# Three edits to a planned kernel: longer planned latencies, mixer loads nine blocks sooner, and a first pair of tiles that runs one tile alone on ten weight slabs

## The chip, the cores and the metric

The kernel runs on all eight cores of one Trainium2 chip. Each core works on one sequence of the batch, and nothing is exchanged between the cores. The metric is the time of one execution on the device, in microseconds (us), of the slowest core.

Executions come in two states. Most are "fast". In some, the cores of one die or of both are granted a lower TensorE clock, and the run is some per cent longer (in the slow run of after one die has 0.960 to 0.965, the other 0.993 to 0.995, and the time is 2481.05 instead of 2411 us; in one run of g2_best_try all eight cores have 0.816 to 0.824, and it takes 2861.9 instead of 2386 us); those are called slow and are left out of every comparison. In some runs that count as fast, two or more cores have a mean granted clock of about 0.98 instead of 0.989 to 0.998, and the run is 10 to 30 us longer. I call those runs "disturbed". I quote the ratio of the fast runs and, beside it, the undisturbed times alone.

## The reference

One layer of a decoder block, for 8 sequences of 4096 positions and width 1024. Every sublayer is modulated by shift, scale and gate rows that come from a conditioning vector `c`.

```python
D_MODEL, BATCH, SEQ, D_FF = 1024, 8, 4096, 2816
def swiglu_ffn(h, w_in, w_out):
    gate, up = jnp.split(h @ w_in, 2, axis=-1)
    return (jax.nn.silu(gate) * up) @ w_out

mod = silu(c) @ w_mod + b_mod                     # 9 rows: sh1, sc1, gt1, sh2, sc2, gt2, sh3, sc3, gt3
h = ada_rmsnorm(x, g_ffn1, sh1, sc1)
x = x + 0.5 * gt1 * swiglu_ffn(h, w_ffn1_in, w_ffn1_out)      # first FFN
h = ada_rmsnorm(x, g_mix, sh2, sc2)               # mixer: conv of width 31 beside a linear recurrence
...                                               # (cut)
x = x + gt2 * (concat(y_conv, y_rnn) @ w_out)
h = ada_rmsnorm(x, g_ffn2, sh3, sc3)
x = x + 0.5 * gt3 * swiglu_ffn(h, w_ffn2_in, w_ffn2_out)      # second FFN
return ada_rmsnorm(x, g_final, f_shift, f_scale)
```

## The kernel before

The sequence is cut into 8 tiles of 512 positions. The first FFN runs on pairs of tiles (pairs 0 to 3), so that each weight slab (128x2048 bf16, 512 KB) serves two tiles. Then each tile runs its mixer and its second FFN.

**A planner of its own.** The kernel lists every operation with a duration and a priority. A list scheduler simulates the engines with these numbers and so fixes, once and for all, the order of instructions on each engine and which buffer each value gets. At run time the engines only follow that order and wait on semaphores. A number such as `DMA_LAT` is thus no delay; it only moves operations in the order. The argument `after` in the listings also acts in the plan alone; `sync` makes an engine wait at run time.

```python
D_CAST, D_SLAB, D_CHUNK, D_PREP = 2.7, 1.65, 0.85, 4.6   # planned us of one DMA channel
DMA_LAT = 2.0
SEM_LAT = 0.08
...
        if op.nbytes:
            ...
                c = max(s + dur, chan[0]) + op.nbytes
                chan[0] = c
                op.end = c + DMA_LAT
        else:
            et[e] = s + sw + dur
            op.end = s + sw + dur + SEM_LAT
...
        for q in op.succ:
            q.ndep -= 1
            q.ready = max(q.ready, op.end if op in q.deps else s)
```

**Weights arrive as fp32.** In pair 0 each slab of `w1i` and `w1o` is loaded by a casting DMA (issued by GpSimd) into one of 10 slab slots, and then written back as bf16 to HBM by a DMA of SyncE; later pairs load the bf16 copy. The weights `w2o` are cast in the same way in the second FFN of tile 0. The others are converted from HBM to HBM during pairs 1 to 3 (the list `prep`).

```python
        def load_slab(nm, r, cast, prio=None, after=(), sync=()):
            b = new(sl, f"{nm}{r}")
            if cast:
                dma("PL", lambda: b.ap, lambda: src, D_CAST, ..., sync=sync)      # cast into the slot
                dma("SP", lambda: d.ap, lambda: b.ap, D_SLAB, ...)                # write back as bf16
            else:
                dma("SP", lambda: b.ap, lambda: d.ap, D_SLAB, ...)
```

**The modulation rows use the same slots.** Eight loads of `wmod` (512 KB each) and eight VectorE operations make one group of eight modulation rows. The groups of sh1 and sc1 come at the start; the VectorE operations of the gate's group (gt1) are planned for after block 8 of pair 0, while its loads are issued as slots come free.

```python
        def mods(m, afters):
            for q in range(8):
                b = new(sl, f"mod{m + q}")
                dma("SP", ..., slab=True, prio=P.prio)                            # wmod row block
                last = A("DVE", 1.3, f, [crow], [b, modr[m]], after=(afters[q],))
...
            for j in range(FC):                                                   # FC = 22 blocks
                slab = load_slab("w1i", j, pi == 0, sync=() if pi else (mod_ops[M_SH1 + 2 * j] if j < 2 else xss[-1][3 if j == 2 else 7].lw,),
                                 after=[xb.lw for xb in xss[-1]] if pi == 0 and j >= 2 else ())
                ops = ffn_in(slab, hbs, hids, j, split=(j == 0))
                anchors.append((pi, ops[-1]))
                if pi == 0 and j == 8:
                    gt_anchor = ops[-1]
...
        def mix_ffn2(t):
            gate_op = (last_in, anchors[-2][1])[t] if t < 2 else ffn_anchor[t - 2]
            xs = load_x(xm_dr, t, after=(gate_op,) * 8)
            ...                                                                   # mixer (cut)
            for j in range(FC):
                slab = load_slab("w2i", j, False)
                ops = ffn_in(slab, [hb2], [hid], j)
            ffn_anchor[t] = ops[-1]
```

`ffn_in` issues, for each tile of the pair, 8 matmuls into a "gate" bank and 8 into an "up" bank of PSUM; ScalarE takes the first bank through SiLU, and a VectorE multiply (`hid`) reads both.

## Time and profile before

| | before |
|---|---|
| time, median of 4 fast runs | 2409.31 us (2407.95 to 2412.9) |
| spans of the eight cores, profiled run | 2386.8 to 2405.7 us |
| TensorE busy, slowest core | 2318.5 us, 96% |

The page of the kernel before begins with the busy time of each engine. Then come 40 equal slices of the span; each digit is the busy share in tenths. "PEclk" is the granted clock.

```profile
span 2405.7 us, 35029 instructions; the slowest of 8 cores (2386.8 to 2405.7 us)
...
PE 2318.5 (96%) x11346; PEld 1110.4 (46%) x11346; DVE 1183.6 (49%) x2019; ACT 931.4 (39%) x1394; POOL 111.2 (5%) x213
...
PE   1999999999999999999899999999999999999997
...
DMA  9999599679867766464976555555555555555455
...
PE 87%; DMA 6%; ACT 3%; DVE 2%; issue 2%; SPq 1%; ACTq 0%; DVEq 0%; POOLq 0%
```

TensorE bounds the kernel: it is busy 96% of the span, and the chain of waits (last line) is 87% matmul. Where the granted clock is 1.00, a 128x512 matmul starts every 0.216 us. What can be won are the few stretches in which TensorE idles or is granted a clock of 0.50 (on core 0, for instance, from 59.5 to 66.2 us, where the matmuls start every 0.427 us), and the chain of the slowest core (core 0) names them. Its columns are start, duration, and what the chain passed through:

```profile
49.84 10.78 DMA sb_slab<-w1i
60.76 115.10 PE ps L443 x520
176.81 39.96 DMA sb_c<-x
...
1182.85 11.17 DMA sb_c<-xmid
```

There are three DMA waits to read here: the third weight slab near 50 us, x of the second pair near 217 us, and x of the third tile's mixer near 1185 us. The waits of TensorE on the same core (total us, times, longest) show the same from TensorE's side; `sb_h` stands for what VectorE makes of the loaded x, and also for the `hid` products:

```profile
PE ps L443 <- DVE sb_h L423: 37.0, 15, 12.4
PE ps L443 <- ACT sb_h L401: 28.9, 2, 28.7
...
PE ps L443 <- DVE sb_c L409: 4.3, 6, 0.8
...
PE ps L443 <- DMA sb_slab<-w1i: 2.9, 1, 2.9
```

For comparing kernels I use one measure that I worked out from the traces, **TensorE's loss** at a time t: the time elapsed minus 0.216 us for each 128x512 matmul and 0.109 us for each 128x256 matmul started so far. It adds up idle time and slow clock and says in which stage they arose. I give its median over those cores of the profiled run whose trace holds all 11346 matmuls and whose clock is at least 0.985. Before, it stands at 55.2 us at 82 us (the start, 45 us, is in it), grows by 5.1 from 82 to 300 us, and by 21.3 from 300 to 2200 us.

### The profile page before, as it was taken

How to read it: one execution, taken by the hardware profiler on the slowest of the kernel's cores; microseconds unless marked ns; L12 is line 12 of the kernel's file. 1: busy time of each engine (PE TensorE's matmuls, PEld its weight loads, DVE VectorE, ACT ScalarE, POOL GpSimd, SP SyncE). 2: the span in 40 equal slices, each digit the busy share in tenths (PEclk: the TensorE clock that was granted, in tenths of full speed). 3: DMA queues.
4: the chain of work that ended last, by engine and by line, in shares of the span. 5: the costliest groups of instructions: out<-in, count | busy, mean ns of one | idle time of the engine just before them, and what ended most of it. 6: DMA issues, size and time to landing. Idle time of an engine off the chain costs nothing.

```text
span 2405.7 us, 35029 instructions; the slowest of 8 cores (2386.8 to 2405.7 us)
## 1 busy us (share of the span) xinstructions
PE 2318.5 (96%) x11346; PEld 1110.4 (46%) x11346; DVE 1183.6 (49%) x2019; ACT 931.4 (39%) x1394; POOL 111.2 (5%) x213
## 2 busy tenths in 40 slices
PE   1999999999999999999899999999999999999997
PEld 0444444444444445454354454454454454454446
DVE  6334133523352337585285385484484584574223
ACT  3214011401131116466265365364364364374222
POOL 0010100010010000000000000000000000000000
PEclk9999999999999999999999999999999999999999
DMA  9999599679867766464976555555555555555455
GB/s 274 226 210 240 176 218 220 166 197 221 218 173 188 187 178 206 153 214 149 225 187 221 189 180 188 187 181 185 191 177 191 186 183 185 186 182 188 162 184 184
DMA packets 135106, 466.64 MB, mean 194 GB/s; under 512 B 16368, under 2 KB 18544, under 8 KB 134256
## 3 DMA queue, kind: packets, MB, share of 16 engines
q1 hardware_dynamic: 117216, 386.54, 49.7%
q0 software_dynamic: 17712, 77.87, 17.3%
q8 instruction: 95, 1.56, 0.3%
q14 instruction: 83, 0.68, 0.1%
HBM read 453.07 MB, written 79.69 MB: 221 GB/s over the span
## 4 chain that ended last, share of the span: by engine, by line
PE 87%; DMA 6%; ACT 3%; DVE 2%; issue 2%; SPq 1%; ACTq 0%; DVEq 0%; POOLq 0%
PE ps L443 87%; DMA sb_c<-x 2%; ACT sb_c L401 2%; DMA sb_c<-xmid 2%; SPq L450 1%; DMA sb_slab<-wmod 1%; DVE sb_c L423 1%; DMA sb_slab<-w1i 0%; DVE sb_c L749 0%; DVE sb_c L409 0%; ACT L401 0%; DVE sb_h L423 0%; DVE sb_c L419 0%; DVE sb_ub L419 0%; DVE sb_c L429 0%
## 5 line engine op out<-in xcount | busy, mean ns | idle before, releaser
L443 PE MATMUL ps<-sb_h,sb_slab 128*128 128x512 bf16 (+1 forms) x10160 | 2178.2, 376 | 31.8 <-ACT sb_h L401 28.9
L443 PEld LDWEIGHTS ps<-sb_h,sb_slab 128*128 128x128 bf16 x10160 | 995.9, 98 | 1195.9 <-issue 44.6
L423 DVE TENSOR_TENSOR sb_h<-ps,sb_c 128x512 bf16<-128x512 f32 x352 | 241.4, 691 | 769.4 <-PE ps L443 708.6
L401 ACT ACTIVATE sb_c<-ps 128x512 f32<-128x512 f32 x400 | 236.5, 596 | 868.0 <-PE ps L443 864.5
L423 DVE TENSOR_TENSOR sb_c<-sb_c 128x512 f32<-128x512 f32 (+1 forms) x492 | 308.8, 672 | 115.6 <-ACT sb_c L401 113.0
L401 ACT ACTIVATE sb_c<-sb_c 128x512 f32<-128x512 f32 (+1 forms) x329 | 198.5, 616 | 263.0 <-DVE sb_c L419 183.3
L401 ACT ACT_TABLE_LOAD x106 | 136.0, 1283 | 224.7 <-PE ps L443 202.4
L419 DVE SCALAR_TENSOR_TENSOR sb_c<-ps,sb_gth,sb_c 128x512 f32<-128x512 f32 (+1 forms) x136 | 96.7, 717 | 212.0 <-PE ps L443 211.6
L401 ACT ACTIVATE sb_h<-sb_c,sb_modv,sb_gs 128x512 bf16<-128x512 f32 x151 | 108.9, 801 | 38.5 <-DVE sb_modv L423 24.9
L443 PE MATMUL ps<-sb_ub,sb_slab 128*128 128x256 bf16 x1024 | 115.0, 273 | 4.9 <-DVE sb_c L409 4.3
L443 PEld LDWEIGHTS ps<-sb_ub,sb_slab 128*128 128x128 bf16 x1024 | 99.5, 98 | 22.1 <-issue 8.7
L500 DVE SCALAR_TENSOR_TENSOR sb_slab<-sb_slab,sb_crow 128x1024 f32<-128x1024 f32 x88 | 107.1, 1217 | 3.4 <-DMA sb_slab<-wmod 2.4
L450 POOL DMA_DIRECT2D y<-sb_c x56 | 30.3, 542 | 1012.9 <-ACT sb_c L401 864.1
L423 DVE TENSOR_TENSOR sb_h<-sb_c 128x512 bf16<-128x512 f32 (+1 forms) x98 | 65.8, 678 | 21.8 <-ACT sb_c L401 19.6
L419 DVE SCALAR_TENSOR_TENSOR sb_c<-sb_ux,sb_vecs,sb_c 128x512 f32<-128x512 f32 x96 | 69.6, 746 | 1.7
L443 PE MATMUL ps<-sb_h,sb_ones 128*128 128x512 bf16 (+1 forms) x98 | 34.4, 382 | 37.3 <-DVE sb_h L423 37.0
L419 DVE SCALAR_TENSOR_TENSOR sb_c<-ps,sb_modv,sb_c 128x512 f32<-128x512 f32 x64 | 47.9, 749 | 31.0 <-PE ps L443 31.0
L419 DVE SCALAR_TENSOR_TENSOR sb_ub<-sb_c,ps 64x256 bf16<-64x256 f32 x128 | 53.8, 420 | 15.1 <-PE ps L443 11.6
L450 POOL DMA_DIRECT2D xmid<-sb_c x64 | 35.0, 547 | 361.6 <-DVE sb_c L419 357.8
L401 ACT ACTIVATE sb_c<-sb_c,sb_lam 128x512 f32<-128x512 f32 x64 | 50.0, 821 | 0.5
L409 DVE TENSOR_SCALAR sb_c<-ps,sb_vecs 64x256 f32<-64x256 f32 x85 | 40.7, 484 | 8.9 <-ACT sb_c L401 4.7
L401 ACT ACTIVATE sb_c<-sb_c,sb_modv,sb_gs 128x512 f32<-128x512 f32 (+1 forms) x65 | 43.6, 751 | 1.2 <-DVE sb_c L423 1.2
(50 smaller groups left out, 454.8 us busy)
## 6 DMA issues: line engine op xcount, KB each, us to landing
sb_slab<-b_w2i SPq DMA_DIRECT2D x176, 512.0 KB, 3.8
sb_slab<-b_w2o SPq DMA_DIRECT2D x96, 512.0 KB, 4.0
sb_slab<-wmod SPq DMA_DIRECT2D x88, 512.0 KB, 8.0
sb_slab<-b_w1i SPq DMA_DIRECT2D x66, 512.0 KB, 8.4
sb_slab<-b_win SPq DMA_DIRECT2D x64, 512.0 KB, 4.4
sb_slab<-b_dcw SPq DMA_DIRECT2D x64, 512.0 KB, 3.8
sb_slab<-b_w1o SPq DMA_DIRECT2D x36, 512.0 KB, 5.8
sb_c<-x SPq DMA_DIRECT2D x64, 256.0 KB, 11.2
```

The source lines that it names most:

```text
L401: return A("ACT", dur, lambda: (lambda o, i: (lambda h: [h.activation(out=o, in_=i, func=func, bias=bias, scale=scale)]))(out(), in_()), r ...
L409: f = lambda: (lambda o, a: (lambda h: [h.tensor_scalar(out=o, in0=a, scalar1=s1, scalar2=s2, op0=op0, op1=op1)]))(out(), in0())
L419: return A("DVE", dur, lambda: (lambda o, a, b: (lambda h: [h.scalar_tensor_tensor(out=o, in0=a, scalar=scalar, in1=b, op0=op0, op1=op1)]) ...
L423: return A("DVE", dur, lambda: (lambda o, a, b: (lambda h: [h.tensor_tensor(out=o, in0=a, in1=b, op=op)]))(out(), in0(), in1()), reads, wr ...
L443: return [h.matmul(o, lhsT=l, rhs=r, start=(first and i == 0), stop=(last and i == n - 1)) for i, (l, r) in enumerate(pr)]
L450: lambda: (lambda o, i: (lambda h: [h.dma_start(out=o, in_=i)]))(out(), in_()),
L500: return lambda h: [h.scalar_tensor_tensor(out=w, in0=w, scalar=1.0, in1=crow.ap, op0=ALU.mult, op1=ALU.mult, accum_out=o)]
```

## The change

Nothing is added to or taken from the work. I call the three parts P, M and S.

- **P, the first pair.** The casts of slabs 2 to 9 no longer wait for x of tile 1. Two casts are in flight, the x blocks of tile 1 come between them, and the write-backs of slabs 0 to 7 wait until tile 1 has used the slab. Since x of tile 1 now comes later, the planner runs tile 0 on ten slabs alone, and then tile 1 on the same ten.
- **M, the mixer loads.** The x loads of the mixer of tile t are let loose (in the plan) at block 12 instead of block 21 of tile t-2's second FFN, and are planned with a latency of 8.0 instead of 2.0.
- **S, the planned latencies.** `SEM_LAT` goes from 0.08 to 0.2; and by a new rule a successor on the same engine counts as ready 0.02 after the end.

```diff
-SEM_LAT = 0.08
+SEM_LAT = 0.2                                                              # S: value
...
-            q.ready = max(q.ready, op.end if op in q.deps else s)
+            t = s if op not in q.deps else op.end - SEM_LAT + 0.02 if op.on == q.eng and not op.nbytes and q.alt is None else op.end
+            q.ready = max(q.ready, t)                                      # S: rule
...
-                if split:
+                if split and hb is hbs[0]:                                 # P
...
             for j in range(FC):
-                slab = load_slab("w1i", j, pi == 0, sync=() if pi else (mod_ops[M_SH1 + 2 * j] if j < 2 else xss[-1][3 if j == 2 else 7].lw,),
-                                 after=[xb.lw for xb in xss[-1]] if pi == 0 and j >= 2 else ())
+                early = pi == 0 and j < 8                                  # P
+                sync = (mod_ops[M_SH1 + 2 * j],) if early and j < 2 else (casts[j - 2],) if pi == 0 and 1 < j < 10 else ()
+                slab = load_slab("w1i", j, pi == 0, sync=sync)
+                casts.append(slab.lw)
+                if early and len(tiles) > 1:
+                    wait_for(x1_loads[j], casts[max(0, j - 3)])
                 ops = ffn_in(slab, hbs, hids, j, split=(j == 0))
+                if early and len(tiles) > 1:
+                    wait_for(slab.wb, ops[-1])
...
-            xs = load_x(xm_dr, t, after=(gate_op,) * 8)
+            xs = load_x(xm_dr, t, after=(gate_op,) * 8, lat=8.0)           # M
...
-            ffn_anchor[t] = ops[-1]
+                if j == 12:
+                    ffn_anchor[t] = ops[-1]                                # M
```

More of the change, by code (lines that the diff above doesn't have):

```diff
@@ L159, in res @@
         return self.fres if self.pool is None else self.pool.res[self.slot]
+DMA_LAT = 2.0
 class Op:
     __slots__ = ("eng", "dur", "fn", "reads", "writes", "prio", "tset", "deps", "succ", "ndep", "ready",
-                 "idx", "nbytes", "sem", "slab", "end", "after", "sync", "tok", "alt", "on")
+                 "idx", "nbytes", "sem", "slab", "end", "after", "sync", "tok", "alt", "on", "lat")
     def __init__(self):
@@ L176, in __init__, with add @@
         self.prio = 0
-    def add(self, eng, dur, fn, reads=(), writes=(), tset=None, nbytes=0, sem=None, slab=None, after=(), prio=None, sync=(), alt=None):
+    def add(self, eng, dur, fn, reads=(), writes=(), tset=None, nbytes=0, sem=None, slab=None, after=(), prio=None, sync=(), alt=None, lat=DMA_LAT):
         op = Op()
+        op.lat = lat
         op.alt = alt
@@ L207 @@
 D_CAST, D_SLAB, D_CHUNK, D_PREP = 2.7, 1.65, 0.85, 4.6
-DMA_LAT = 2.0
-SEM_LAT = 0.08
+SEM_LAT = 0.2
 SWITCH = 1.4
@@ L308, in schedule @@
                 chan[0] = c
-                op.end = c + DMA_LAT
+                op.end = c + op.lat
         else:
@@ L446, in mms, with dma @@
             return A("PE", mm_us(n, cols), f, reads, [bank], prio=prio)
-        def dma(q, out, in_, nbytes, sem, reads, writes, slab=None, after=(), prio=None, sync=()):
+        def dma(q, out, in_, nbytes, sem, reads, writes, slab=None, after=(), prio=None, sync=(), lat=DMA_LAT):
             return A(q, 0.06 if q == "SP" else 0.3,
                      lambda: (lambda o, i: (lambda h: [h.dma_start(out=o, in_=i)]))(out(), in_()),
-                     reads, writes, nbytes=nbytes, sem=sem, slab=slab, after=after, prio=prio, sync=sync)
+                     reads, writes, nbytes=nbytes, sem=sem, slab=slab, after=after, prio=prio, sync=sync, lat=lat)
         dr = lambda d, r: d[r * 128:(r + 1) * 128, :]
@@ L464, in load_slab @@
                 d = scr[nm][r]
-                dma("SP", lambda: d.ap, lambda: b.ap, D_SLAB, lambda: wb_sems[b.slot], [b], [d], prio=prio)
+                b.wb = dma("SP", lambda: d.ap, lambda: b.ap, D_SLAB, lambda: wb_sems[b.slot], [b], [d], prio=prio)
             else:
@@ L523, in build_program, with load_x @@
         tsc(k_(bah.ap), k_(V[:, V_BA:V_BA + 8]), 0.5, None, ALU.mult, None, [vecs], [bah], dur=0.17)
-        def load_x(src, t, prio=None, after=(None,) * 8):
+        def load_x(src, t, prio=None, after=(None,) * 8, lat=DMA_LAT):
             xs = []
@@ L530, in load_x @@
                 d = src[t][f]
-                dma("SP", lambda b=b: b.ap, lambda d=d: d.ap, D_CHUNK, slot_sem(b), [d], [b], prio=prio, after=(after[f],))
+                dma("SP", lambda b=b: b.ap, lambda d=d: d.ap, D_CHUNK, slot_sem(b), [d], [b], prio=prio, after=(after[f],), lat=lat)
                 xs.append(b)
@@ L612, in ffn_out, with wait_for @@
             return done
+        def wait_for(op, other):
+            op.sync.append(other)
+            op.deps.add(other)
         pairs = [list(range(p, min(p + 2, n_tiles))) for p in range(0, n_tiles, 2)]
@@ L626, in build_program @@
                 xss = [load_x(x_dr, t, prio=-26 if t == 0 else -15, after=[None if t == 0 else sh1_last] * 8) for t in tiles]
+                x1_loads = [b.lw for b in xss[-1]]
                 hbs = [norm(xs, M_SC1, M_SH1, prio=-23 if t == 0 else 300) for t, xs in zip(tiles, xss)]
@@ L631, in build_program @@
             hids = [[] for _ in tiles]
-            next_in = []
+            next_in, casts = [], []
             for j in range(FC):
-                slab = load_slab("w1i", j, pi == 0, sync=() if pi else (mod_ops[M_SH1 + 2 * j] if j < 2 else xss[-1][3 if j == 2 else 7].lw,),
-                                 after=[xb.lw for xb in xss[-1]] if pi == 0 and j >= 2 else ())
+                early = pi == 0 and j < 8
[4 more added lines that the diff above has]
+                    wait_for(x1_loads[j], casts[max(0, j - 3)])
                 ops = ffn_in(slab, hbs, hids, j, split=(j == 0))
+                if early and len(tiles) > 1:
+                    wait_for(slab.wb, ops[-1])
                 anchors.append((pi, ops[-1]))
```

## The prediction

> **What bounds it now.** TensorE: the page has it busy 2318.5 of 2405.7 us (96%), and the chain of waits is 87% matmul. A warm 128x512 matmul starts every 0.216 us. Only its idle and slow-clock stretches can be won. On the slowest core (core 0) the timeline and the waits show:
> 1. First FFN matmul at 45.8 us, after the last modulation row (landed 43.0).
> 2. 54.5–60.8 us: 6 us idle. The third weight slab's cast was issued only at 49.84, after x of tile 1, and landed at 60.6. Then 13 matmuls run at 0.427 us. From 45.8 to 66 TensorE loses about 10.5 us.
> 3. 215.6–223: about 5 us, for x of the next pair (issued 176.8, landed 216.8; DMA share 1.0 from 20 to 235 us).
> 4. 1185–1199: 10.8 us at the third tile's mixer. Its x loads are issued at 1178–1183 and take 7 to 11 us beside the casts of w2o.
> 5. 0.8 to 1.8 us at each later mixer (6 us together), 1.0 us each at six more places, a tail of 15 us.
>
> [...]
>
> **What the change does.** No arithmetic, bytes or matmuls are added or removed; only order, gates and planned latencies.
> - First pair: slabs 2 to 9 no longer wait for x of tile 1; two casts are in flight, x comes between. The order of TensorE shows tile 0 on ten slabs (34 us), then tile 1 on the same. Casts with a write-back beside them landed 4.5 us apart; with write-backs held back I estimate 3 us plus 0.8 per x block, which keeps up with 3.45 us per slab. Item 2 shrinks from 10.5 to 2–4 us: gain 7. Item 1 stays within 1–2 us: x was queued behind the modulation rows.
> - The price: those write-backs wait for tile 1's matmuls (from about 85 us). The DMA queue loses some 10 us of use between 75 and 88, and the same bytes are wanted by about 210. Item 3 grows from 5 to 8–12 us: I give back 4.
> - Mixer loads: issued after block 12 instead of 21, nine blocks or 31 us sooner, against a load of 5–11 us. Item 4 goes (gain 10), and item 5's waits for x (gain 5).
> - Longer planned latencies reorder the streams; perhaps 1 us.
>
> Sum on core 0: 7 − 4 + 10 + 5 + 1 = 19. Faster cores have less to win, so the spread narrows.
>
> **Prediction: 2390 us, 8 in 10 between 2376 and 2402.** Faster by over 2%: 2%; within 2%: 96%; slower by over 2%: 2%.
>
> **What would show it.** Right: no gap of TensorE between 50 and 80 us; casts of slabs 2–9 about 3–4 us apart; no wait near 1185; xmid landed well before its use; a wait of 5–12 us near 205–220. Wrong: TensorE waiting for a cast at each of the first ten slabs; or new waits for ACT or DVE in the mixers, which now start inside the blocks of the second FFN.
>
> **What would make it wrong.** Cast latency with two in flight above 7 us (TensorE starves, +10 to +20 us); a larger stall at item 3; or no stall there at all (2375).

What the trace of before shows, on core 0: from 59.5 to 66.2 us, after the waits of 2.8 and 2.9 us, the granted clock is 0.50 and the matmuls start every 0.427 us, against 0.216 at 1.00. These slow starts are in the 10.5 us of item 2. The spacing of 3 us plus 0.8 per x block is my estimate, not a measurement; in the trace of after it came to 4.1 us. And the DMA share of item 3 is not 1.0 throughout: it is 0.83 from 100 to 120 us.

## The result, and the profile after

| | before | after |
|---|---|---|
| fast runs | 2407.95 to 2412.9 (4) | 2410.8, 2410.86, 2411.69 (a fourth, 2481.05, was slow) |
| median of all runs | 2409.31 us | 2411.28 us |
| spans of the cores, profiled run | 2386.8 to 2405.7 | 2396.9 to 2409.3 |

The ratio of after to before is 1.0005 (95%: 0.9986 to 1.0025): the same. Ratios are the mean time of one kernel's fast runs over that of the other's of the same rounds, so they are not quite the ratio of the medians. The gain of 19 us that I forecast is not there.

The page after (the trace of this core misses some 200 matmul records, so its busy time of TensorE is a little low):

```profile
span 2409.3 us, 34716 instructions; the slowest of 8 cores (2396.9 to 2409.3 us)
...
PE 2304.4 (96%) x11139; PEld 1111.0 (46%) x11346; DVE 1193.7 (50%) x2012; ACT 932.7 (39%) x1397; POOL 111.3 (5%) x213
...
PE   2988999999999999999999999999999999999997
...
PE 79%; DMA 9%; DVE 5%; ACT 3%; issue 3%; SPq 1%; DVEq 0%; ACTq 0%; POOLq 0%; POOL 0%
```

The first slice of TensorE went from 1 to 2 and the twentieth, near 1185 us, from 8 to 9: those are the two intended gains. The third and the fourth slice (120 to 241 us) went from 9 to 8: that is new loss. In the chain DVE grew from 2% to 5%. The waits of TensorE on core 0 after, against those shown of before:

```profile
PE ps L447 <- DVE sb_h L427: 39.0, 14, 12.8
PE ps L447 <- ACT sb_h L405: 28.2, 1, 28.2
...
PE ps L447 <- DVE sb_ub L423: 8.7, 8, 1.3
...
PE ps L447 <- DMA sb_slab<-b_wout: 4.4, 1, 4.4
PE ps L447 <- DMA sb_slab<-w1i: 0.3, 1, 0.3
```

The wait for the third slab fell from 2.9 to 0.3 us. But the largest total, for `sb_h`, did not fall although the wait at 1185 us is gone; and two waits are new: eight for `sb_ub` and one for `b_wout`. To see where these lie I go to core 5, whose matmul records are complete in all the traces that I set side by side. Three stretches of 20 us (columns: stretch, its length, busy us and count of PE, PEld, DVE, ACT, POOL, then granted clock, DMA share and GB/s), before:

```profile
60.00:80.00 20.00, 17.22 (x69) 7.23 (x70) 8.42 (x14) 10.61 (x14) 0.00 (x0) 0.83 1.03 194
160.00:180.00 20.00, 20.00 (x95) 9.02 (x94) 3.79 (x6) 3.58 (x6) 1.58 (x3) 1.00 1.04 218
220.00:240.00 20.00, 17.70 (x70) 7.59 (x71) 14.20 (x23) 14.48 (x21) 2.70 (x5) 0.83 1.02 283
```

The same stretches of core 5 after:

```profile
60.00:80.00 20.00, 20.00 (x94) 8.93 (x93) 13.22 (x23) 11.42 (x16) 2.11 (x4) 1.00 1.01 181
160.00:180.00 20.00, 13.46 (x54) 5.65 (x55) 7.27 (x13) 1.79 (x3) 2.11 (x4) 0.76 1.03 217
220.00:240.00 20.00, 11.30 (x44) 4.71 (x43) 9.65 (x17) 11.41 (x15) 1.08 (x2) 0.74 0.75 209
```

Read the matmul counts: 25 more in the first stretch, 41 fewer in the second, 26 fewer in the third. At 0.216 us each that is 5.4 us won, then 8.9 and 5.6 us lost. The stall of the third stretch existed before and grew; that of the second did not exist at all.

**The new stall at 157 us.** Here is TensorE of core 5 after (start, duration, what, and the idle time before it with what ended it):

```profile
138.81 18.29 PE L447 MATMUL ps<-sb_h,sb_slab 128*128 128x512 bf16 x84
166.21 5.32 PE L447 MATMUL ps<-sb_h,sb_slab 128*128 128x512 bf16 x16 [9.10 <-DVE sb_h L427]
```

It waits 9.1 us for VectorE, which therefore should be working hard. VectorE of the same core shows the opposite:

```profile
155.22 1.22 DVE L504 SCALAR_TENSOR_TENSOR sb_slab<-sb_slab,sb_crow 128x1024 f32<-128x1024 f32 x1 [5.64 <-DMA sb_slab<-wmod]
...
164.23 1.23 DVE L504 SCALAR_TENSOR_TENSOR sb_slab<-sb_slab,sb_crow 128x1024 f32<-128x1024 f32 x1 [7.78 <-DMA sb_slab<-wmod]
...
165.38 0.69 DVE L427 TENSOR_TENSOR sb_h<-ps,sb_c 128x512 bf16<-128x512 f32 x1
...
169.24 1.23 DVE L504 SCALAR_TENSOR_TENSOR sb_slab<-sb_slab,sb_crow 128x1024 f32<-128x1024 f32 x1 [3.18 <-DMA sb_slab<-wmod]
```

VectorE idles 7.78 us for a modulation row (L504) of the gate, and right behind it in its fixed order stands the `hid` multiply (L427), which frees the PSUM banks that TensorE needs; 0.14 us after its end TensorE goes on. The multiply itself waited for nothing that was late: the last operation of ScalarE before it ended at 157.91 us and TensorE idled from 157.1 us, yet it starts at 165.38 us, behind the row. The 16 matmuls after the gap take 5.32 us, which is 0.33 us each instead of 0.216: the granted clock is 0.50 from 159.5 to 169.6 us, and up to then they start 0.38 to 0.43 us apart.

The chain of core 5 after shows how late the row was:

```profile
141.55 27.52 DMA sb_slab<-wmod
195.39 33.42 DMA sb_c<-x
...
1230.28 26.43 DMA sb_slab<-b_wout
```

The last row took 27.52 us from issue to landing (169.1 us). In the kernel before the last row of this group landed at 124.4 us on the same core. About half of these 45 us is a later issue (141.55 instead of 119.42 us), the other half a slower landing (27.52 instead of 4.94 us). The three lines of this chain are the three new or larger stalls: at 157, at 222 (x of the second pair, landed 228.8 us, before 225.3) and at 1250.

### The profile page after: what moved, and what is told of

The parts are those of the page before. It is cut to its first block, busy times and chain, and to the rows that moved or that the text cites. A ratio compares the mean times of both kernels' runs of the same rounds, so it can differ in the third digit from the quotient of the medians.

```text
span 2409.3 us, 34716 instructions; the slowest of 8 cores (2396.9 to 2409.3 us)
## 1 busy us (share of the span) xinstructions
PE 2304.4 (96%) x11139; PEld 1111.0 (46%) x11346; DVE 1193.7 (50%) x2012; ACT 932.7 (39%) x1397; POOL 111.3 (5%) x213
## 4 chain that ended last, share of the span: by engine, by line
PE 79%; DMA 9%; DVE 5%; ACT 3%; issue 3%; SPq 1%; DVEq 0%; ACTq 0%; POOLq 0%; POOL 0%
PE ps L447 79%; DMA sb_slab<-wmod 2%; DMA sb_slab<-w1i 2%; ACT sb_c L405 2%; DMA sb_c<-x 1%; DMA b_w1i<-sb_slab 1%; ACT L405 1%; DMA sb_slab<-b_wout 1%; DVE sb_c L423 1%; DMA sb_slab<-w1o 1%; DVE sb_ub L423 1%; DVE sb_c L413 1%; DMA sb_slab<-w2o 1%; SPq L454 1%; DVE sb_c L764 1%
## 5 line engine op out<-in xcount | busy, mean ns | idle before, releaser
L427 DVE TENSOR_TENSOR sb_h<-ps,sb_c 128x512 bf16<-128x512 f32 x352 | 241.5, 691 | 677.0 <-PE ps L447 599.4
L427 DVE TENSOR_TENSOR sb_c<-sb_c 128x512 f32<-128x512 f32 (+1 forms) x492 | 310.5, 673 | 94.7 <-ACT sb_c L405 90.9
L405 ACT ACTIVATE sb_h<-sb_c,sb_modv,sb_gs 128x512 bf16<-128x512 f32 x160 | 116.4, 807 | 29.3 <-DVE sb_modv L427 24.4
L504 DVE SCALAR_TENSOR_TENSOR sb_slab<-sb_slab,sb_crow 128x1024 f32<-128x1024 f32 x88 | 107.2, 1218 | 33.3 <-DMA sb_slab<-wmod 32.3
L427 DVE TENSOR_TENSOR sb_h<-sb_c 128x512 bf16<-128x512 f32 (+1 forms) x98 | 66.2, 677 | 16.3 <-ACT sb_c L405 12.8
```

Of the source, the lines that this page charges most:

```text
L405: return A("ACT", dur, lambda: (lambda o, i: (lambda h: [h.activation(out=o, in_=i, func=func, bias=bias, scale=scale)]))(out(), in_()), r ...
L427: return A("DVE", dur, lambda: (lambda o, a, b: (lambda h: [h.tensor_tensor(out=o, in0=a, in1=b, op=op)]))(out(), in0(), in1()), reads, wr ...
L504: return lambda h: [h.scalar_tensor_tensor(out=w, in0=w, scalar=1.0, in1=crow.ap, op0=ALU.mult, op1=ALU.mult, accum_out=o)]
```

## The experiments

Undisturbed times are given in the table below. The runs fell on six chips: A the comparison of before and after above; B e1 to e4; C f1, f3, m_mixer_only and m_first_pair_only; D g1 to g3 and m2_mixer_only; E h1, h2 and g4; F i1. The undisturbed times of the kernel before were 2408 to 2413 us on A (4 runs), 2415 to 2417 on B (3), 2417.5 on D (1), 2408 to 2414 on E (4) and 2414 to 2422 on F (6); on C there were none. So between chips the same kernel moves by some 10 us, and only differences on one chip, or in one stage of the trace, are to be trusted below that. Before and after were traced on chip A only, so a comparison of losses is also one between chips. All sixteen runs below gave correct results.

The last three columns are TensorE's loss (as defined above): at 82 us, and what was added from 82 to 300 us and from 300 to 2200 us.

| run | parts and additions | undisturbed times, us | ratio to before [95%] | loss at 82 | 82–300 | 300–2200 |
|---|---|---|---|---|---|---|
| before | – | 2407.95–2412.9 | – | 55.2 | 5.1 | 21.3 |
| after | P M S | 2410.8–2411.7 | 1.0005 [0.9986, 1.0025] | 47.8 | 19.1 | 16.5 |
| e1_old_first_pair | M S | 2411.0, 2411.5 | 0.996 [0.9877, 1.0042] | 55.4 | 9.8 | 18.9 |
| e2_no_defer | P M S, write-backs not held | 2416.1–2418.5 | 0.9952 [0.9839, 1.0064] | 60.6 | 11.3 | 17.6 |
| e3_gt_late | P M S, gate rows planned late | 2393.2–2394.5 | 0.9855 [0.9769, 0.9941] | 50.0 | 0.8 | 18.7 |
| e4_gt_x_late | e3, and x of pair 1 planned late | 2392.8–2394.8 | 0.9856 [0.9784, 0.9928] | 48.4 | 0.3 | 14.7 |
| f1_hold_casts | P M S, casts 16–19 held | 2410.1–2416.4 | 0.9925 [0.9815, 1.0034] | 49.3 | 15.2 | 19.8 |
| f3_gt_late_w2o_prep | e3, and w2o converted early | 2407.4, 2408.0 | 0.9921 [0.9808, 1.0034] | 48.8 | 21.3 | 15.7 |
| m_mixer_only | M | 2398.1 | 0.9895 [0.9642, 1.0148] | 55.0 | 8.2 | 8.8 |
| m2_mixer_only | M | 2399.2 | 0.991 [0.9829, 0.999] | 55.3 | 8.7 | 12.2 |
| m_first_pair_only | P | 2422.6, 2424.4 | 1.0022 [0.9847, 1.0197] | 49.4 | 22.2 | 20.5 |
| g1_no_sem | P M | 2405.4–2409.1 | 0.9871 [0.9812, 0.9931] | 50.0 | 22.9 | 10.8 |
| g3_x_late | P M S, x of pair 1 planned late | 2401.4–2407.3 | 0.9861 [0.981, 0.9911] | 48.6 | 9.3 | 21.0 |
| g2_best_try | P M, both planned late | 2385.9–2386.9 | 0.9787 [0.9728, 0.9846] | 50.6 | 2.3 | 11.0 |
| h1_rule_only | P M, rule of S | 2412.1–2413.1 | 0.9967 [0.9895, 1.0039] | 48.2 | 19.1 | 21.9 |
| h2_value_only | P M, value of S | 2405.1–2408.3 | 0.9926 [0.9859, 0.9993] | 53.3 | 15.1 | 6.6 |
| g4_best_w2o_prep | g2, w2o early, later gate anchor | 2381.3–2385.7 | 0.9828 [0.9762, 0.9895] | 49.6 | 4.6 | 5.0 |
| i1_best_value | g4, with the value of S | 2380.6–2385.0 | 0.9855 [0.9829, 0.9881] | 55.2 | −0.1 | 2.9 |

### First round: is the stall a matter of order or of DMA capacity?

My theory (A) was that the first pair simply shifted the same bytes to later and that capacity limits it. The rival (B) was that the order is at fault: rows that nobody needs yet compete with casts that nobody needs yet.

**e1_old_first_pair** undoes P and keeps M and S (the main lines of its edit):

```diff
-                sync = (mod_ops[M_SH1 + 2 * j],) if early and j < 2 else (casts[j - 2],) if pi == 0 and 1 < j < 10 else ()
-                slab = load_slab("w1i", j, pi == 0, sync=sync)
+                slab = load_slab("w1i", j, pi == 0, sync=() if pi else (mod_ops[M_SH1 + 2 * j] if j < 2 else xss[-1][3 if j == 2 else 7].lw,),
+                                 after=[xb.lw for xb in xss[-1]] if pi == 0 and j >= 2 else ())
...
-                if early and len(tiles) > 1:
-                    wait_for(slab.wb, ops[-1])
```

> The changed kernel with the first pair put back as it was before (mixer loads and planned latencies stay changed). Theory A (the first pair's new order wins 8 us before 82 us and loses 11 us near 157 and 5 us more near 222 than before, so it is a net loss of about 8 us, while the mixers' part wins 5 to 8 us): 2400 to 2405 us, ratio to before about 0.997, no wait near 157, the gap near 55 to 61 us back. Rival B (the first pair is neutral, and the mixers' part brings nothing because the stall near 1185 only moved to 1250): 2408 to 2412 us, ratio 1.000.

Measured: 2411.0 and 2411.5 us undisturbed; TensorE's loss at 82 us is back at 55.4. From 82 to 300 us it adds 9.8 instead of 19.1. So the first pair as changed wins 7.6 us by 82 us and pays 9.3 us until 300: it returns all that it wins. What M and S bring without P is less clear: this run is 4 to 6 us under the undisturbed runs of before on the same chip, but its loss at 2200 us is 2.5 us above that of before (84.1 against 81.6, traced on two chips). Both are less than the 15 us that I had put down for M alone, so P is not the whole story.

**e2_no_defer** deletes only the wait of the write-backs:

```diff
-                if early and len(tiles) > 1:
-                    wait_for(slab.wb, ops[-1])
```

> The changed kernel without the rule that the write-backs of the first eight slabs wait for tile 1's matmuls. Theory A (holding the write-backs back leaves the DMA queue idle from about 66 to 88 us, and the debt makes the late modulation rows and x of the next pair land about 10 us later): the stall near 157 goes below 4 us and the x stall near 222 shrinks to 3 to 6 us; casts of slabs 2 to 9 land 4.5 us apart instead of 3.8 and TensorE loses up to 8 us before 90 us; total 2398 to 2406 us. Rival B (tile 0 alone needs the whole DMA for its casts, so early write-backs cost more than they give): TensorE waits for a cast at several of the first ten slabs, 10 us or more, total 2410 us or above. Rival C (the stalls come from the fixed order of DVE alone): stall near 157 unchanged.

Measured: 2416.1 to 2418.5 us, level with before on this chip (2415 to 2417) and, in TensorE's loss at 2200 us, 6 us worse than after (89.5 against 83.4). TensorE of core 5 from 40 to 120 us waits once 14.4 us, which does not exist in after (there 2.1):

```profile
PE ps L447 <- ACT sb_h L405: 29.0, 2, 27.7
PE ps L447 <- DVE sb_h L427: 17.6, 2, 14.4
PE ps L447 <- DMA sb_slab<-w1i: 2.1, 1, 2.1
```

The 14.4 us are not for a cast: a statistics matmul of tile 1 waits for the last x block of tile 1, issued at 63.09 and landed at 85.5 us (in after at 66.3), in the very stretch that the change wants to speed up. The casts of slabs 2 to 9 landed 5.6 us apart instead of 4.1, but only one is waited for (2.1 us). The holding has a price as well, which the columns of the table hide because they part at 82 us: at 140 us the loss is 69.5 us here and 47.8 in after, while from 140 to 300 us it grows by 2.4 us here and by 19.1 in after. So the holding gains some 22 us early and some 17 of them come due later. This run does not say how much of the 17 is spared only because TensorE is already late.

**e3_gt_late** changes one planned number, the latency of the gate rows' loads. No wait and no anchor is touched:

```diff
                 dma("SP", lambda b=b: b.ap.bitcast(F32), lambda s=src: s, D_SLAB, slot_sem(b), [], [b], slab=True,
-                    prio=P.prio)
+                    prio=P.prio, lat=30.0 if m == M_GT1 else DMA_LAT)
```

> The changed kernel with one planned latency longer: the weight rows of the first gate's modulation are planned at 30 us, which puts their DVE operations later in DVE's fixed order; nothing else is asked for. Theory A (the 157 stall is DVE blocked in its fixed order on those rows; but TensorE is then paced by x of the next pair, which lands near 229 us): the stall near 157 goes (under 2 us), the stall near 222 grows by 6 to 11 us, total unchanged within 3 us (2408 to 2413 us). Rival B (the two stalls add): the stall near 222 stays at 8 to 10 us and the total falls by about 10 us, to 2400 us. Rival C (the 157 stall is a starved cast): it stays.

Measured: 2393.2 to 2394.5 us, 17 us less than after had on chip A, and 21 to 24 less than the undisturbed runs of before on this chip. The loss added from 82 to 300 us falls from 19.1 to 0.8. All that is left of TensorE's waits of core 5 from 84 to 300 us, where after has three of 18.1 us in total, is this:

```profile
PE ps L447 <- DMA sb_slab<-w1i: 0.8, 1, 0.8
```

Its two stretches of core 5 that were bad in after:

```profile
160.00:180.00 20.00, 19.15 (x90) 8.54 (x88) 10.38 (x17) 3.58 (x6) 4.66 (x9) 1.00 1.02 207
220.00:240.00 20.00, 20.00 (x94) 9.08 (x93) 8.92 (x14) 6.51 (x10) 3.26 (x6) 1.00 1.02 235
```

The DMA engines are as busy as in after from 160 to 180 us (1.02 against 1.03) and move no more (207 against 217 GB/s), yet TensorE runs through. That settles capacity against order: theory A, that the total would not move, is wrong. B is right that it falls, but not in why it falls so far: the stall near 222 us, which B expected to stay, went too. The landings on core 5 show what the number did. Rows planned to end late hold their slab slots longer in the plan, so the casts that follow (17th slab on) are issued from 155.8 us instead of from 143.4 us; the last row lands at 157.6 instead of 169.1 us, and the last x of the second pair at 208.1 instead of 228.8 us.

**e4_gt_x_late** adds the same to x of the second pair, which moves its statistics matmuls later in TensorE's order:

```diff
-                xss = [load_x(x_dr, t, prio=lp, after=prev_in[8 * (t % 2):8 * (t % 2) + 8]) for t in tiles]
+                xss = [load_x(x_dr, t, prio=lp, after=prev_in[8 * (t % 2):8 * (t % 2) + 8], lat=30.0 if pi == 1 else DMA_LAT) for t in tiles]
```

> As the run before, and x of the second pair is also planned at 30 us, which puts the last statistics matmul of the second pair 88 matmuls (19 us) later in TensorE's order, into the output blocks of the first pair. Theory A (both stalls are fixed order against late transfers; no engine is short of time): both go, TensorE's loss until 300 us falls from about 68 to 48 to 55 us, total 2390 to 2397 us. Rival B (the DMA engines are the limit until 240 us): the stall moves to the casts or write-backs of the output weights between 225 and 290 us and the total stays above 2404 us.

Measured: 2392.8 to 2394.8 us, the same as e3. With the rows out of the way x is in time already, and there is nothing left to win there.

### Second round: what delays the rows, and do the mixers win what they should?

e3 moves both the order of VectorE and the DMAs. One explanation (Q) is that rows land late because casts that are not needed yet share the 16 DMA engines. Another (R) is that only the place of the row operations in VectorE's order counts.

**f1_hold_casts** keeps the rows' place in VectorE's order nearly as it was (in the trace two or three operations earlier), and holds casts 16 to 19 until block 14 is done:

```diff
+                if pi == 0 and 16 <= j < 20:
+                    wait_for(slab.lw, end14)
                 ops = ffn_in(slab, hbs, hids, j, split=(j == 0))
+                if j == 14:
+                    end14 = ops[-1]
```

> The changed kernel with four casts (slabs 16 to 19) held until TensorE has ended slab 14; planned latencies are those of the changed kernel, and the eight gate-modulation operations stand in DVE's order within one or two places of where they stood there. It tells apart why the longer planned latency of the run before won 17 us. Theory Q (the hardware DMA queue was slowed by casts that were not yet needed, so rows and x of the next pair came late; the longer plan helped because it held slots and with them the casts): the last modulation row lands by about 160 instead of 169 us, the last x by 215 instead of 228; stall near 157 falls from 11 to 6 us or less, stall near 222 is gone; total 2397 to 2403 us. Theory D (only the place in DVE's order matters): the stall near 157 stays at 9 us or more and the stall near 222 stays too; total 2408 to 2413 us.

Measured: 2410.1 to 2416.4 us, no gain in total. The two largest waits of TensorE on core 5 from 84 to 300 us:

```profile
PE ps L447 <- DVE sb_h L427: 11.3, 2, 10.6
PE ps L447 <- DMA sb_slab<-w1i: 1.1, 1, 1.1
```

The stall at 157 us is all but gone (0.7 us of waiting for `sb_h` from 140 to 180 us, after 9.4), and the rows have landed by 151.0 us, with 10.6 to 19.6 us each instead of 10.2 to 27.5 in after. So rows that come sooner are enough: with no row operation moved later in VectorE's order, the stall went. That they came sooner because fewer casts shared the DMA engines, as Q says, is shown only in part: the held casts also changed the order in which slots are handed out, and of the 18 us by which the last row landed sooner, 10 are an earlier issue (131.44 instead of 141.55 us) and 8 a quicker landing (19.59 instead of 27.52 us). R is not refuted: in e3 the eight row operations stand eight or nine `hid` multiplies later in VectorE's order than in after. The stall at 222 us stays, 10.6 us: once let go, ten casts were issued between 155.7 and 162.5 us, and x of the second pair landed at 223.7 us behind them. Holding the burst moved it onto the next victim.

The trace of after shows how crowded these engines were. From 140 to 170 us on core 5 the two DMA queues of the page took 53.2% and 48.1% of the 16 engines, together all of them. Rows issued by SyncE take up to 27.5 us there beside casts issued by GpSimd, while bf16 slabs of the same size, loaded by SyncE in the second FFNs, take 3.8 us (median of the loads of `b_w2i` before, core 0, where the DMA share is 0.55 from 1400 to 2300 us).

**m_mixer_only** is the kernel before with M alone. **m_first_pair_only** is the kernel before with P alone.

```diff
-            xs = load_x(xm_dr, t, after=(gate_op,) * 8)
+            xs = load_x(xm_dr, t, after=(gate_op,) * 8, lat=8.0)
...
-            ffn_anchor[t] = ops[-1]
+                if j == 12:
+                    ffn_anchor[t] = ops[-1]
```

> The kernel before with only the mixers' part of the change: x loads after block 12 and planned at 8 us; first pair and semaphore latencies as before. Theory A (the gain at the third tile's mixer, 5 to 10 us by core, is paid back by 1 to 2 us at each of the first mixers and by a wait of 3 to 8 us near 1250 us, where the casts of the last output weights now stand beside the output projection's weights): within 4 us of before, a wait for wout near 1250, TensorE's loss from 900 to 1300 us about 11 us instead of 9 to 15. Rival B (the mixers' part alone keeps its gain and the other two parts eat it): 2398 to 2402 us where before has 2409, no wait for wout.

> The kernel before with only the first pair's part of the change; mixers and planned semaphore latencies as before. Theory A (as in the changed kernel it wins 8 us by 82 us and pays 9 to 12 us near 157 and 4 to 8 us more near 222): TensorE's loss until 300 us 65 to 70 us instead of 58 to 65, total 2410 to 2417 us. Rival B (the later stalls came from the new semaphore latencies): loss until 300 us 50 to 56 us, total 2400 us.

Measured: M alone gave 2398.1 us in its one undisturbed run, P alone 2422.6 and 2424.4 us. In the loss, M alone adds 8.8 us from 300 to 2200 us against 21.3 before, so it wins about 12; P alone wins 5.8 by 82 us and then adds 22.2 instead of 5.1 until 300: it loses about 11 net. TensorE's waits of core 5 from 900 to 1300 us with M alone begin with:

```profile
PE ps L447 <- DMA sb_slab<-b_wout: 2.9, 1, 2.9
```

This wait was not there before (there the largest of that stretch is 2.6 us for `sb_h`). It has the same kind of cause as the stalls of the first pair. Before, 8 of the 12 casts of `w2o` were issued from 1144.7 to 1188.7 us, well ahead of the four `b_wout` loads of this mixer (1238.6 to 1247.9). With x in time, the mixer no longer waits and is placed ahead of that work: in after all 12 casts are issued from 1208.6 to 1251.9 us, and the `b_wout` loads (1215.4 to 1230.3) among them, beside the write-backs. They took 14.6 to 26.4 us; before they took 11.4 to 13.9. With M alone the picture is the same (casts from 1197.9, `b_wout` 14.3 to 23.0 us).

**f3_gt_late_w2o_prep** is e3 with `w2o` converted ahead from HBM to HBM, like the other weights:

```diff
-        prep = [(nm, r) for nm in ("win", "dcw", "wout", "w2i") for r in range(len(scr[nm]))]
+        prep = [(nm, r) for nm in ("win", "dcw", "wout", "w2i", "w2o") for r in range(len(scr[nm]))]
...
-                    slabs = [load_slab("w2o", 3 * q + s, t == 0 and cs.start == 0) for s in range(3)]
+                    slabs = [load_slab("w2o", 3 * q + s, False) for s in range(3)]
```

> The kernel with the gate rows planned at 30 us (2394 us), and besides the last output weights are converted during the first FFN with the other weights, so no casts stand near 1210 to 1280 us. Theory A (the wait near 1250 us is the output projection's weights queued behind those casts and their write-backs): the wait is gone, TensorE's loss from 1200 to 1300 us falls from 7 to 8 us on the slow cores to 2 to 3, total 2386 to 2391 us. Rival B (the wait is the fixed order of the slabs): it stays, total 2394 us; and the 12 more conversions may slow the first FFN's loads (DMA share 0.75 to 0.98 there), which would show as new waits between 300 and 900 us.

Measured: 2407.4 and 2408.0 us, 14 us worse than e3 instead of better. In its own stage theory A holds: the wait for `b_wout` is gone, and from 1200 to 1300 us the loss grows by 2.0 to 2.3 us on the six cores counted, where in e3 it grows by up to 8.2. But this edit far downstream changed the plan of the first pair: the gate rows were now issued before casts that were due, and TensorE of core 5 waits 6.6 us for a slab of `w1i` and 9.3 us for x; the loss adds 21.3 us from 82 to 300 us. In total the run is a miss, and a warning: in a planned kernel an edit in one place moves instructions elsewhere, so one has to look at every stage before one credits the edit.

### Third round: is it S?

With the first pair mended, the mixers still add 18.7 us in e3, and 8.8 with M alone. What differs is S.

**g1_no_sem** is after without S; **m2_mixer_only** repeats M alone on this chip.

```diff
-SEM_LAT = 0.2
+SEM_LAT = 0.08
...
-            t = s if op not in q.deps else op.end - SEM_LAT + 0.02 if op.on == q.eng and not op.nbytes and q.alt is None else op.end
+            t = s if op not in q.deps else op.end
```

> The changed kernel with only the planned semaphore latency and its same-engine rule put back. Theory A (that part costs 2 to 2.5 us near 950 to 1000 us and 4 to 5 us from 1300 to 2200 us): total 2399 to 2404 us; loss from 1300 to 2200 us 4 to 5 us instead of 9; stalls near 157 and 222 as in the changed kernel. Rival B (neutral): 2409 to 2412 us.

> The run m_mixer_only again, on another chip and with more rounds, as its only undisturbed time (2398.1 us) stood beside no undisturbed run of before. If the trace of that run is right (loss from 1300 to 2200 us 4 to 5 us, where before has 9 to 12; near 1185 us nothing): 2396 to 2400 us, ratio 0.994 to 0.997. If it was an accident: 2405 to 2410 us.

Measured: g1 takes 2405.4 to 2409.1 us and adds 10.8 us from 300 to 2200 us, where after adds 16.5. In the first pair it is the other way: 22.9 against 19.1. M alone takes 2399.2 us again, in its one undisturbed run, with 12.2 us added from 300 to 2200 us (the trace is of a disturbed run; the limit of 0.985 leaves out the two cores concerned).

**g3_x_late** is after with only the second half of e4, x of pair 1 planned late:

> The changed kernel with only x of the second pair planned at 30 us: its last statistics matmul stands 88 matmuls (19 us) later in TensorE's order. Theory A (the stall near 222 is TensorE's fixed order against x that lands at 228 us): the stall near 157 stays at 8 to 11 us, the one near 222 falls from 8 to 11 us to 0 to 2, total 2399 to 2404 us. Rival B (TensorE then runs into late casts of the output weights): a new wait of the same size between 225 and 290 us, total 2408 us or above.

Measured: 2401.4 to 2407.3 us. The stall at 222 us is gone and that at 157 stays, on core 5:

```profile
PE ps L447 <- DVE sb_h L427: 6.8, 1, 6.8
```

So the two stalls have separate handles: x needs a later place in TensorE's order, or rows and casts that come at the right time.

**g2_best_try** is after without S, with both late plans of e4:

> A version meant to beat both: the changed first pair and mixer loads, planned semaphore latency back at 0.08 us as before, gate rows and x of the second pair planned at 30 us. Theory A (the longer planned semaphore latency costs about 8 us in the mixers, the two late transfers cost 20 us in the first pair): TensorE's loss until 300 us 48 to 53 us, growing by only 8 to 12 us from 900 to 2200 us; total 2378 to 2386 us. Rival B (the semaphore latency is neutral): same as with it, 2392 to 2396 us.

Measured: 2385.9 to 2386.9 us, 7 us under e3 and e4, though on another chip (D instead of B; the undisturbed runs of before are alike on the two). The first pair adds 2.3 us from 82 to 300, the mixers 11.0.

### Fourth round: which half of S, and the best version

**h1_rule_only** (`SEM_LAT` back at 0.08, the rule kept) and **h2_value_only** (0.2, the rule removed):

```diff
 h1:
-SEM_LAT = 0.2
+SEM_LAT = 0.08
 h2:
-            t = s if op not in q.deps else op.end - SEM_LAT + 0.02 if op.on == q.eng and not op.nbytes and q.alt is None else op.end
+            t = s if op not in q.deps else op.end
```

> The changed kernel with the planned semaphore latency put back to 0.08 us, but the new rule for successors on the same engine kept (they are planned 0.02 us after their producer). The order of TensorE again puts 12 filler matmuls between the seventh and eighth gate matmul of the first mixer. Theory A (the value 0.2 makes the plan's orders for the mixers worse): loss from 1300 to 2200 us 4 to 6 us as without the whole part; total 2400 to 2407 us. Theory B (the rule does it): loss from 1300 to 2200 us 8 to 10 us, waits of 1.1 to 1.3 us for DVE's writes of ub at every mixer, total 2408 to 2413 us.

> The other half: 0.2 us for every successor, also on the same engine. Theory A (the value does it): loss from 1300 to 2200 us 8 us or more; total 2408 us or above. Theory B (the rule does it): 4 to 6 us. Neither theory says anything of the first pair here; its order moves too (39 instead of 48 matmuls before the first statistics of tile 1).

Measured on the same chip: the rule alone takes 2412.1 to 2413.1 us, the value alone 2405.1 to 2408.3 us. From 300 to 2200 us the rule adds 21.9 us, the value 6.6. TensorE's waits of core 5 from 1300 to 2400 us, in after (all) and then with the rule alone (the two largest):

```profile
PE ps L447 <- DVE sb_ub L423: 5.4, 5, 1.3
PE ps L447 <- DVE sb_h L427: 4.1, 6, 1.7
```

```profile
PE ps L447 <- DVE sb_ub L423: 5.2, 5, 1.3
PE ps L447 <- DVE sb_c L413: 3.7, 10, 0.5
```

With the value alone the waits for `sb_ub` are not there, and this is the whole list:

```profile
PE ps L447 <- DVE sb_h L427: 2.9, 6, 1.9
```

The five waits for `sb_ub` (the input of the convolution, which VectorE writes) come with the rule, one in each mixer of that stretch: on core 5 all nine traces with the rule have them and none of the nine without. With P and M in place the four combinations add, from 300 to 2200 us, 10.8 us (neither, g1), 21.9 (the rule), 6.6 (the value) and 16.5 (both, after). So the rule costs 10 to 11 us with or without the value, and the value wins 4 to 5 us with or without the rule; the traces are from three chips. The rule makes a chain on one engine look cheap in the plan, so the planner sets other work elsewhere; that this is how the waits arise is argued from the plan and not shown by itself. The value has a price of its own in the first pair: h2 waits once 11.8 us there for a group of modulation rows, and its loss at 82 us is 53.3 instead of 47.8.

**g4_best_w2o_prep** is g2 with `w2o` converted ahead (as in f3) and the operations of the gate rows planned for after block 13 instead of 8, which keeps the first pair's order sound despite the changed plan. **i1_best_value** is g4 with the value of S and without its rule.

```diff
-                if pi == 0 and j == 8:
+                if pi == 0 and j == 13:
                     gt_anchor = ops[-1]
```

> The fastest version so far (2386 us) with the last output weights converted during the first FFN, so that no casts stand at 1205 to 1280 us; the gate rows' operations are asked for after block 13 instead of 8, because this takes them back to within five places of where they stood in DVE's order. Theory A (the wait of 3 to 5 us near 1245 us on the slow cores is wout behind the casts of w2o): no wait for wout, loss from 1200 to 1300 us 1 to 3 instead of 4 to 7 us on cores 1, 2, 3, 5 and 7; total 2379 to 2384 us if the first pair keeps its loss of 48 to 55 us. Rival B (it is the order of slabs): the wait stays, 2386 us.

> The fastest version (2382 us) with the planned semaphore latency at 0.2 us again, but without the same-engine rule: the half of that part which the last runs showed to help the mixers. If the two add: loss from 900 to 2200 us 3 to 4 us instead of 5 to 6, first pair 50 to 58 us until 300, total 2376 to 2384 us. If the other order of the first pair (39 matmuls before tile 1's first statistics) costs what it cost in h2_value_only (4 to 5 us by 82 us): 2382 to 2387 us, no better.

Measured: g4 takes 2381.3 to 2385.7 us (5 undisturbed runs, median 2382.2), where the undisturbed runs of the kernel before on that chip took 2408.3 to 2414.1: about 1.2% faster. i1 takes 2380.6, 2381.1 and 2385.0 us, where before took 2414.2 to 2422.4 on that chip: about 1.5%. Both beat before; after, which on chip A took as long as before, was not run beside them. Between them I can't choose: they ran on two chips, and their times overlap. In g4 all that TensorE of core 5 waits from 900 to 1300 us is this, with no `b_wout` and no `sb_ub`:

```profile
PE ps L447 <- DVE sb_c L413: 0.3, 1, 0.3
PE ps L447 <- ACT sb_h L405: 0.2, 1, 0.2
```

## Why the prediction was wrong, point by point

The prediction was 2390 us with a range of 2376 to 2402; measured were 2411. Its sum was 7 − 4 + 10 + 5 + 1 = 19 us won. In TensorE's loss the change won 7.4 by 82 us, lost 14.0 from 82 to 300 us (19.1 against 5.1), and won 4.8 from 300 to 2200 us (16.5 against 21.3): −1.8 in all, which fits the measured +2 us of the medians.

- **"Item 2 shrinks from 10.5 to 2–4 us: gain 7": right.** Loss at 82 us 55.2 before, 47.8 after. The casts of slabs 2 to 9 landed 51.1 to 80.1 us on core 5, 4.1 us apart on the average; I had estimated 3 to 4. "Item 1 stays within 1–2 us" was right too.
- **"Item 3 grows from 5 to 8–12 us: I give back 4": right for the stall at 222 us, wrong for the first pair. This is the step that failed most.** From 200 to 250 us TensorE's loss grows by 9.2 us after and by 5.3 before, so this stall did cost 4 us more (the wait there is 6.1 to 9.9 us on the eight cores, and the slow clock after it comes on top: on core 5 it is 0.50 from 224.4 to 234.5 us). But from 140 to 200 us the loss grows by 9.9 us after and not at all before. What the step left out is this second victim of the held-back transfers: the gate's modulation rows, 45 us later than before, with VectorE's fixed order behind them and TensorE behind that. The waits at 157 us are 3.4 to 9.4 us on the eight cores. So the term "give back 4" was in truth 14. I had looked at the DMA queue as bytes that are wanted by 210 us, and not at each transfer that TensorE's order depends on. e3 shows that no bytes had to move faster: by one planned number the price of 14 turns into a gain of 4 (0.8 against 5.1).
- **"Item 4 goes (gain 10)": right as far as it goes.** The wait at 1185 us is gone. A new one of 3.2 us (core 5; 4.4 on core 0) for `b_wout` came 65 us later, because the mixer that no longer waits now runs into the casts of `w2o`, of which two thirds had been done ahead of it before. I hadn't asked what the mixer would meet once it came sooner.
- **"and item 5's waits for x (gain 5)": not in after.** The mechanism was right: M alone wins 9.1 to 12.5 us from 300 to 2200 us, against the 15 that I had for items 4 and 5 together. In after the waits for x in the later mixers are gone (on core 0 before, 0.6 to 1.6 us at five of them), but waits for `sb_ub` stand in their place, 8.7 us in total on core 0. I had named "new waits for ACT or DVE in the mixers" as a sign of being wrong, but for another reason (the earlier start); M alone doesn't show them.
- **"Longer planned latencies reorder the streams; perhaps 1 us": wrong in sign.** With M present, the runs without any of S add 8.8 to 12.2 us from 300 to 2200 us (g4 aside, where `w2o` is converted early), those with all of S 14.7 to 21.0. In this stage S costs about 6 us (16.5 in after against 10.8 in g1; 4 to 10 in the other pairs that differ in S alone), half of what M wins. Its rule is the culprit (21.9 against 6.6 with the value alone, same chip). I had treated a change of planner constants as noise, although it touches every engine's order in every stage.
- **"Faster cores have less to win, so the spread narrows": right**, 2386.8 to 2405.7 became 2396.9 to 2409.3; but it narrowed because the fast cores lost.

What stays open: the parts don't add up exactly. In the first pair S improves P (82–300: 19.1 with S, 22.9 without), and without P it costs about 1 (9.8 against 8.2 and 8.7). Each combination is another static order, and I can't separate a law from luck with it. Why the value of S gives i1 a perfect stretch from 82 to 300 us and yet costs 5 us before 82 us I did not follow up. The loss before 300 us of runs with the same order varies by a few us from core to core; no run here shows why.

## What to carry to other kernels

When you move loads earlier or hold some back, list every transfer that shares the DMA engines in the next 100 us, and ask of each which engine, in its fixed order, stands behind it: the victim here was not the data that was moved but a modulation row in front of a PSUM-freeing multiply. When the plan is fixed beforehand, planning a transfer late is a cheap tool: one number took 14 us out of TensorE's loss (at 2200 us 69.5 in e3 against 83.4 in after), while holding DMAs by waits only moved the burst (f1). Test planner constants as a part of their own, by stage, since a change that wins in one stage can hide a loss in another.

## What the runs showed of the chip

- A load of 512 KB had no single time. In the second FFNs it took 3.8 us (`b_w2i` before, issued by SyncE), but under a backlog the same size took 27.5 us (a row, 141.55 to 169.07 us, after, core 5) and 26.4 us (`b_wout`, the same trace), and a cast to 512 KB from fp32 up to 34.1 us (before, core 0).
- Eight cores are 96 to 97% busy on TensorE (before, profiled run), and the cores of the undisturbed runs are granted 0.989 to 0.998 on the average of the run. In the slow runs the lowest clock of a core reached 0.814, in runs of 2868 to 2870 us of M alone. So the load alone did not hold the cores at the lower clock; why most executions of one program escape it is open.
- In the two traces of the state that I call disturbed, TensorE is granted 0.81 from about 234 to 395 us on two cores (their mean over the run is 0.981 to 0.982), busy for at least 158.9 of the 160 us from 235 to 395 on cores 6 and 7 of e1_old_first_pair, and 1.00 afterwards. At 0.81 a stretch of 160 us costs about 30 us, an estimate from these figures (0.19 of 160). The runs take 10 to 30 us longer (for instance 2430.9 to 2442.7 us in three runs of the kernel before on one chip). In one run labelled slow it stood alone, on four cores, at 2442.9 us. What starts and ends it is open.
- One late operand in VectorE's fixed order kept TensorE idle for 9.1 us (after, core 5, at 157 us).
